# Gate-up groups of a hybrid encoder layer: the order written in the source, and shared banks added in ahead of the last pair

## The chip, the cores and the metric

The kernel runs on one core of a Trainium2 chip. The metric is the device time of one execution in microseconds (us), as the median of several runs; lower is better. Five engines work side by side, each on its own queue of instructions: TensorE (PE; its weight loads are shown apart as PEld), VectorE (DVE), ScalarE (ACT), GpSimd (POOL) and SyncE (SP). Here SP starts nearly all transfers from HBM; POOL starts those that add to what is in SBUF.

## What is computed

One encoder layer in float32, for 256 tokens of width 2048. The change touches the two feed-forward blocks, and of these the first product.

```python
def swiglu(x, w_gate_up, w_down):
    gate, up = jnp.split(x @ w_gate_up, 2, axis=-1)
    return (jax.nn.silu(gate) * up) @ w_down

ff = swiglu(rms_norm(x, pre_norm_ffn1[layer]), w_ffn1_gate_up[layer], w_ffn1_down[layer])
x = x + 0.5 * rms_norm(ff, post_norm_ffn1[layer])
h = rms_norm(x, pre_norm_mix[layer])
... # one projection, a bidirectional recurrence and windowed attention, one projection back
ff = swiglu(rms_norm(x, pre_norm_ffn2[layer]), w_ffn2_gate_up[layer], w_ffn2_down[layer])
x = x + 0.5 * rms_norm(ff, post_norm_ffn2[layer])
```

`w_gate_up` is 2048 x 11264 (gate and up, 5632 columns each), `w_down` 5632 x 2048. All of this is read from HBM once per execution.

## The kernel before

**Three products for one.** TensorE multiplies in a rounded form of float32. Each float32 operand is therefore split into a high part `h` (ScalarE casts it, L176) and a residual `l` (VectorE subtracts, L177), and a product is the sum of three: high by high, high by residual, residual by high. `three` issues these (L442); each multiplies 128 x 128 by 128 x 512. The split of half a raw tile (128 x 1024) is `split_half`; the rings `hip` and `lop` hold five such halves each.

**Groups and pairs.** `Gated` computes gate and up for 512 columns at a time: a group, 11 of them (0 to 10). In a group the contraction over 2048 runs over 8 pairs (u = 0 to 7) of two 128-row slices. The weights of a pair are one raw tile of 128 x 2048 (1 MB, two transfers of 512 KB): four blocks, called b11, b12, b21, b22, two rows k by the columns of gate and of up (n). The results of a group are four PSUM banks `c[m][n]`, with m the half of the tokens; two are of the tag `pa`, two of `pb`, and each tag has four banks.

**Plain and seven-product pairs.** A plain pair makes 8 block products, 24 instructions of TensorE. A pair in `MIXED_IN` makes seven block products instead (Strassen's scheme in Winograd's form), 21 instructions: sums of weight blocks by sums of activations. Two of the seven go straight into c00 and c01, one into c10, and four into shared banks p1, p5, p6, p7, which all such pairs of the group add to. Once in a group `fold` makes from the four shared banks what is still to be added to each of the four c banks: one copy on ScalarE (L530) and eight additions on VectorE (L524 to L547). It does so inside the last pair, whose products are sorted by bank: one addition into a bank, then that bank's six products. With two rooms (`rooms == 2`) the last reads of p5 come late in it (L528). Groups 2 to 10 have four seven-product pairs (2, 3, 4, 6), group 1 has two (2 and 3), since the activation sums of the others are made while it runs; group 0 has none.

**Prepared pairs.** For a seven-product pair, `prepare` runs three or four places ahead (`LEADS`): it loads the raw tile, splits b11 (a short cast and a short residual, 128 x 512), and has POOL start a transfer that reads the other half of the weights a second time and adds it to the first in SBUF (L906). When the pair's turn comes, `seven` splits the lower half, makes two more additions of blocks (L482, L484), splits the upper half, and splits the lower half again. Raw tiles of prepared pairs take turns in three buffers (`rawp`), those of plain pairs in two (`gated.room`).

**After a group** `units` multiplies the silu of the scaled gate (L1017, ScalarE) by the scaled up (L1018, VectorE), transposes the result on TensorE (eight short instructions, L1029, into one bank of each tag), and splits it into `ht`; for the first 8 tiles it also keeps sums of the blocks (`sums_of`, L395 to L399). Its first half runs at the end of the group, its second inside pair 1 of the next one. `put_away` stores some tiles `ht` to HBM from group 2 to 5.

**The order.** Outside of regions marked `manual_schedule`, a planner at build time places every instruction on its engine's queue, by the order in the source as a priority and by its own costs of instructions. The gate-up groups are left to it. Each engine then runs its queue in that order.

Of the kernel before, what the change touches and what calls it, by code (L numbers as in the profile page):

```python
# [20 lines left out]
P = 128  # L21
# [3 lines left out]
KT = D // P  # L25
# [12 lines left out]
def hymba_layer_kernel(  # L38
# [363 lines left out]
    class Blocks:  # L402
# [7 lines left out]
        def __init__(self, tiles, sums):  # L410
            self.tiles, self.sums = tiles, sums
            self.prepared = {}
# [51 lines left out]
        def seven(self, u, aside=None):  # L464

            ready = self.prepared.pop(u, None)
            raw = ready[0] if ready else load(self.source(u))
# [4 lines left out]
            if ready:  # L472
                h, l = ready[1:]
            else:
                h, l = self.one_block()
                split_act(h, l, b11)

                nc.vector.tensor_tensor(
                    four[:, 0:2], four[:, 0::3], four[:, 1:2].to_broadcast([P, 2, 512]), ALU.add
                )  # L480
            lower = split_half(raw, 1)
            nc.vector.tensor_tensor(b22, b11, b22, ALU.add)  # L482
            if ready:
                nc.vector.tensor_tensor(b21, b22, b21, ALU.add)  # L484
            upper = split_half(raw, 0)
            if not ready:
                nc.vector.tensor_tensor(b21, b22, b21, ALU.add)
            if aside:
                aside()
            last = split_half(raw, 1)  # L490
            if not self.p:
# [12 lines left out]
            for at, left, right in (  # L504
                (("p", 0), lhs(0, 0), (h, l)),
                (("c", 0, 0), lhs(1, 0), rhs(lower, 0)),
                (("c", 0, 1), summed(S4), rhs(lower, 1)),
                (("p", 1), summed(S1), rhs(upper, 0)),
                (("p", 3), summed(S3), rhs(upper, 1)),
                (("p", 2), summed(S2), rhs(last, 1)),  # L510
                (("c", 1, 0), lhs(1, 1), rhs(last, 0)),
            ):
                self.three(at, *left, *right)
# [35 lines left out]
        def load_plain(self, u):  # L549
            return load(self.source(u))  # L550

# [7 lines left out]
        def work(self, upto, among=None):  # L559


            while self.pos < upto:
# [8 lines left out]
                else:  # L571
# [4 lines left out]
                    else:  # L576
                        hs, ls = split(self.load_plain(u))
# [276 lines left out]
    MIXED_IN = (2, 3, 4, 6)  # L854
    LEADS = (4, 4, 4, 3)
# [7 lines left out]
    class Gated(Blocks):  # L863
# [7 lines left out]
        def group(self, g, c=None):  # L871
            self.g = g
            self.begin(range(KT // 2), c)

# [7 lines left out]
        def load_plain(self, u):  # L882
            if self.g == 0:
                return load(self.source(u))
            return load(self.source(u), pool=self.room, bufs=2)

        def prepare(self):

            for at, lead in zip(MIXED_IN, LEADS):
                g = self.g  # L890
                if at < lead:
                    at, g = at - lead + KT // 2, g + 1
                else:
                    at -= lead
                u = (at + lead) % (KT // 2)
                if at != self.pos - 1 or g >= NG:
                    continue
                if u not in (self.mixed if g == self.g else self.sums):
                    continue
                src = self.source(u, g)  # L900
                raw = load(src)
                h, l = (
                    self.room.tile([P, 512], F32R, tag=t, name=nm(t), bufs=3) for t in ("h1", "l1")
                )
                split_act(h, l, raw[:, 0:512])
                nc.gpsimd.dma_start(  # L906
                    raw[:, 0:1024].rearrange("p (k c) -> p k c", k=2),
                    src[:, :, 1],
                    accum_op=ALU.add,
                )  # L910
                self.prepared[u] = raw, h, l
# [27 lines left out]
    def ffn(gated, w_dn, post_gain, again, gain=None, lead=None, aside=None):  # L939

        with ExitStack() as st:
# [59 lines left out]
            def folded():  # L1001
                a, b = room_for("z"), room_for("s")
                if gated.g < NG - 1:
                    gated.rooms = 2
                    return [[a, b], [a, b]]
                gated.rooms = 4
                wide = work.tile([P, 2, 512], F32, tag="sp", name=nm("y"), bufs=3)
                return [[a, b], [wide[:, i, :] for i in range(2)]]

            gated.folded = folded  # L1010

            def units(c, scale):

                zs = []
                for m in range(2):
                    z = room_for("zs"[m])
                    nc.scalar.activation(z, c[m][0], AF.Silu, scale=scale[:, m : m + 1])  # L1017
                    nc.vector.scalar_tensor_tensor(  # L1018
                        z, c[m][1], scale[:, m : m + 1], z, ALU.mult, ALU.mult
                    )  # L1020
                    zs.append(z)
                yield
                for j in range(2):
                    bank = (pa, pb)[j]()
                    for i in range(2):
                        for m in range(2):
# [4 lines left out]
                            )  # L1031
                    g = len(hts)
# [11 lines left out]

            pre_stats()
            waiting = None
            for g in range(NG):
                if g:
                    gated.group(g)
                for u in range(gated.pos, KT // 2):  # L1050
                    gated.work(u + 1, (lambda: next(waiting)) if waiting and u == 1 else None)
                    if g == 0:
                        if u == 4:
                            power_and_rest()
                            spread(two)
                        for done in {4: (0, 1, 2), 5: (3, 4), 6: (5, 6), 7: (7,)}.get(u, ()):
                            even(done)
                            if done in MIXED_IN[:2]:
                                sums_in(done)
                        if u == 5 and aside:  # L1060
                            aside()
                    if g == 1 and u in (5, 6):
                        sums_in(MIXED_IN[u - 3])
                    if u == 4 and 1 < g <= AWAY // 2 + 1:
                        put_away(2 * g - 4)
                        put_away(2 * g - 3)
                    gated.prepare()
                waiting = units(gated.c, rest if g else rs2)
                next(waiting)
# [14 lines left out]
            rows.work(2, lambda: next(waiting))  # L1084
# [639 lines left out]
```

## Time and profile before

| | |
|---|---|
| median of 3 runs | 1942.75 us (1942.46 to 1943.67) |
| profiled execution, its own time | 1941.62 us |
| span of the profiled execution | 1939.8 us |
| mean granted TensorE clock | 0.981 |
| bytes moved by DMA | 422.42 MB, 218 GB/s on average |
| packets' time, as a share of 16 DMA engines: started by SP / by POOL | 55.5% / 12.9% |

In lists of waits a row reads: engine, line, what it waited for, microseconds in all, times, the longest. In a timeline a row gives start and duration, and in brackets the idle time ahead of it with what ended it. Rows of instruction groups read: line, engine, operation, out<-in, shapes, count, then busy time and mean nanoseconds of one, then idle time ahead of them and what ended it. In a table of windows each row is a stretch of the span with every engine's busy time, the granted clock (PEclk), the mean busy share of the DMA engines and GB/s.

### The profile page before, as it was taken

What the parts mean: (1) busy time and instruction counts of PE and PEld (TensorE: products, weight loads), DVE (VectorE), ACT (ScalarE), POOL (GpSimd) and SP (SyncE); (2) the same over time, 40 slices, a digit from 0 to 9 for tenths busy, and PEclk for the clock granted to TensorE, in tenths of its full rate; (3) what the DMA queues carried; (4) which work ended last, traced back from release to release, by engine and by line L of the source; (5) the groups of instructions that cost most, each with busy time, mean ns of one, the idle gap of its engine ahead of it and who ended that gap; (6) DMA issues with size and microseconds to landing.
All of it is one profiled execution on the core that took longest, in us unless ns stands there. A gap on an engine that the chain in (4) does not pass through costs nothing.

```text
span 1939.8 us, 23224 instructions
## 1 busy us (share of the span) xinstructions
PE 1859.2 (96%) x8438; PEld 1523.5 (79%) x8438; DVE 1612.7 (83%) x2071; ACT 1113.9 (57%) x1492; POOL 114.4 (6%) x115
## 2 busy tenths in 40 slices
PE   9998899999999999999999999999899989999998
PEld 6776777777788888888888888877777777788886
DVE  7877788887899999667687798977788888899997
ACT  6454555554566566576577566554555555656564
POOL 1100011000000000000000000100000001000000
PEclk9999999999999999999999999999999999999999
DMA  8877777777665566665555457877877777775565
GB/s 295 234 231 227 227 223 225 217 221 215 213 262 204 209 237 234 206 195 156 181 163 157 180 215 253 244 234 230 226 220 214 223 219 219 207 280 196 211 217 190
DMA packets 200019, 422.42 MB, mean 218 GB/s; under 512 B 10984, under 2 KB 45888, under 8 KB 199136
## 3 DMA queue, kind: packets, MB, share of 16 engines
q1 hardware_dynamic: 178880, 380.95, 55.5%
q0 software_dynamic: 21024, 39.99, 12.9%
q8 instruction: 66, 1.08, 0.2%
q14 instruction: 49, 0.40, 0.1%
HBM read 408.29 MB, written 12.60 MB: 217 GB/s over the span
## 4 chain that ended last, share of the span: by engine, by line
PE 58%; DVE 16%; DMA 14%; ACT 7%; issue 4%; POOL 0%; SPq 0%; ACTq 0%; DVEq 0%; POOLq 0%
PE pa L442 22%; PE pb L442 19%; DMA raw<-in_w_ffn_gate_up_dram 13%; DVE l L177 9%; PE pa L309 5%; ACT h L176 5%; PE pa L314 3%; PE pa L364 2%; PE pa L362 2%; PE pa L363 2%; DVE raw L484 1%; DMA raw<-in_w_ffn_down_dram 1%; DVE ht L177 1%; DVE raw L482 0%; DVE s L528 0%
## 5 line engine op out<-in xcount | busy, mean ns | idle before, releaser
L176 ACT CAST h<-raw 128x1024 fp32r<-128x1024 f32 (+1 forms) x861 | 838.0, 1011 | 616.7 <-DMA raw<-in_w_ffn_gate_up_dram 262.2
L177 DVE TENSOR_TENSOR l<-raw,h 128x1024 fp32r<-128x1024 f32 (+1 forms) x861 | 984.7, 1173 | 242.2 <-ACT h L176 214.7
L442 PE MATMUL pa<-h,xt 128*128 128x512 f32 x1104 | 401.8, 406 | 22.0 <-DVE s L528 19.1
L442 PE MATMUL pb<-h,xt 128*128 128x512 f32 x952 | 348.1, 400 | 0.2 <-DVE z L524 0.2
L442 PEld LDWEIGHTS pa<-h,xt 128*128 128x128 f32 x1104 | 215.8, 196 | 77.1 <-DVE s L528 24.9
L442 PE MATMUL pa<-l,xt 128*128 128x512 f32 x552 | 223.4, 405 | 0.0
L442 PEld LDWEIGHTS pb<-h,xt 128*128 128x128 f32 x952 | 183.9, 193 | 39.3 <-DVE z L524 0.6
L442 PE MATMUL pb<-l,xt 128*128 128x512 f32 x476 | 189.0, 397 | 0.0
L442 PE MATMUL pb<-h,ht 128*128 128x512 f32 x464 | 163.5, 390 | 0.0
L442 PE MATMUL pa<-h,ht 128*128 128x512 f32 x464 | 163.1, 389 | 0.0
L442 PE MATMUL pb<-h,xs 128*128 128x512 f32 x304 | 112.4, 401 | 32.8 <-ACT h L176 32.7
L906 POOL DMA_DIRECT2D raw<-in_w_ffn_gate_up_dram x76 | 92.2, 1213 | 851.8 <-DVE l L177 748.0
L442 PEld LDWEIGHTS pa<-l,xt 128*128 128x128 f32 x552 | 108.5, 197 | 24.4 <-DVE l L177 1.9
L309 PE MATMUL pa<-xt,h 128*128 128x512 f32 x512 | 124.5, 393 | 0.2 <-ACT h L176 0.2
L309 PEld LDWEIGHTS pa<-xt,h 128*128 128x128 f32 x512 | 93.8, 188 | 18.7 <-ACT h L176 0.6
L442 PEld LDWEIGHTS pb<-l,xt 128*128 128x128 f32 x476 | 91.6, 192 | 18.9
L442 PE MATMUL pa<-h,xs 128*128 128x512 f32 x304 | 105.9, 389 | 0.0
L442 PEld LDWEIGHTS pa<-h,ht 128*128 128x128 f32 x464 | 87.1, 188 | 18.2
L442 PEld LDWEIGHTS pb<-h,ht 128*128 128x128 f32 x464 | 87.1, 188 | 18.1
L442 PEld LDWEIGHTS pb<-h,xs 128*128 128x128 f32 x304 | 57.8, 190 | 50.3 <-ACT h L176 40.2
L442 PE MATMUL pa<-l,ht 128*128 128x512 f32 x232 | 90.4, 390 | 0.0
L442 PE MATMUL pb<-l,ht 128*128 128x512 f32 x232 | 90.3, 389 | 0.0
(283 smaller groups left out, 2538.7 us busy)
## 6 DMA issues: line engine op xcount, KB each, us to landing
raw<-in_w_ffn_gate_up_dram SPq DMA_DIRECT2D x350, 512.0 KB, 6.1
raw<-in_w_ffn_down_dram SPq DMA_DIRECT2D x88, 1024.0 KB, 5.3
raw<-in_w_mix_in_dram SPq DMA_DIRECT2D x52, 1024.0 KB, 5.1
raw<-in_w_ffn_gate_up_dram POOLq DMA_DIRECT2D x76, 512.0 KB, 6.0
raw<-in_w_mix_out_dram SPq DMA_DIRECT2D x16, 1024.0 KB, 5.0
away<-ht SPq DMA_DIRECT2D x16, 512.0 KB, 6.0
ht<-away SPq DMA_DIRECT2D x16, 512.0 KB, 7.0
pg<-in_post_norm_ffn_dram SPq DMA_DIRECT2D x4, 512.0 KB, 7.3
```

The source lines that it names most:

```text
L176: nc.scalar.copy(hi, src)
L177: nc.vector.tensor_tensor(lo, src, hi.bitcast(F32), ALU.subtract)
L309: nc.tensor.matmul(slot[f], weights(hs, kk, f), xcol(xt, k), start=(k == 0), stop=(k == KT - 1))
L314: nc.tensor.matmul(slot[f][:, 0:T], weights(ls, kk, f), xcol(xt, kh * 8 + kk, 0), start=False, stop=False,)
L362: nc.tensor.matmul(dst, xh, h[:, o : o + n], start=(k == 0), stop=False)
L363: nc.tensor.matmul(dst, xh, l[:, o : o + n], start=False, stop=False)
L364: nc.tensor.matmul(dst, xl, h[:, o : o + n], start=False, stop=(k == KT - 1))
L442: nc.tensor.matmul(self.bank(at), lhs, rhs, start=(n == 1), stop=n in (ends, self.of[at]), skip_group_check=n > ends,)
L484: nc.vector.tensor_tensor(b21, b22, b21, ALU.add)
L906: nc.gpsimd.dma_start(raw[:, 0:1024].rearrange("p (k c) -> p k c", k=2), src[:, :, 1], accum_op=ALU.add,)
```

## The change

The groups from 1 on are issued inside `manual_schedule`, which fixes on every engine the order in which the source issues instructions. The source therefore now writes that order out.

- `plan` lists all pairs of groups 1 to 10 in two kinds, mixed (seven-product) and plain, and loads three mixed and two plain raw tiles. Afterwards `load_next` issues the next load of a kind as soon as the last split of a tile of that kind is issued.
- `splits` issues a pair's splits in steps, `take` gives or issues its products. In most of the group (`pair_ahead`) the first two splits of pair u + 1 stand ahead of the products of pair u, and the third behind them.
- `prepare` of the four mixed pairs stands, in this order: for the first, while pair 6 of the group before is at work; for the second and third, in `first_pairs` before the products of pair 0; for the fourth, ahead of the products of pair 3.
- `boundary` takes the place of the fold inside the last pair, with one order written out for ScalarE, VectorE and TensorE: the additions into c00 and c10 come first, and p5 is read for the last time ahead of the addition into c11. The first split of the next group's pair 0 stands between the additions.
- `units` has finer steps: the two silus at the boundary, the multiplications at the start of the next group, the transposes behind pair 0, the evacuation among the splits of pair 2.
- The seven-product pairs are 2, 4, 5 and 6, and in group 1 they are 2 and 4.

The last group's fold is written apart and keeps four rooms. `seven` loses its branch for prepared pairs, and its products become a function of their own, `products`.

```diff
-    MIXED_IN = (2, 3, 4, 6)
-    LEADS = (4, 4, 4, 3)
+    MIXED_IN = (2, 4, 5, 6)
...
+        def plan(self):
+            self.here = {g: MIXED_IN if g > 1 else MIXED_IN[:2] for g in range(1, NG)}
+            self.kinds = {True: [], False: []}
+            for g in range(1, NG):
+                for u in range(KT // 2):
+                    self.kinds[u in self.here[g]].append((g, u))
+            self.raws, self.firsts, self.split_of = {}, {}, {}
+            for mixed in (False, True, False, True, True):
+                self.load_next(mixed)
+
+        def load_next(self, mixed):
+            if self.kinds[mixed]:
+                g, u = self.kinds[mixed].pop(0)
+                kw = {} if mixed else {"pool": self.room, "bufs": 2}
+                self.raws[g, u] = load(self.source(u, g), **kw)
...
+        def splits(self, g, u):
+            raw = self.raws[g, u]
+            got = self.split_of[g, u] = []
+            if (g, u) in self.firsts:
+                b11, b12, b21, b22 = (raw[:, i * 512 : (i + 1) * 512] for i in range(4))
+                got.append(split_half(raw, 1))
+                nc.vector.tensor_tensor(b22, b11, b22, ALU.add)
+                nc.vector.tensor_tensor(b21, b22, b21, ALU.add)
+                yield
+                got.append(split_half(raw, 0))
+                yield
+                got.append(split_half(raw, 1))
+                self.load_next(True)
+            else:
+                got.append(split_half(raw, 0))
+                yield
+                got.append(split_half(raw, 1))
+                self.load_next(False)
+            yield
...
+            def boundary(g):
+                a, b = room_for("z"), room_for("s")
+                c, (p1, p5, p6, p7) = gated.c, gated.p
+                add = nc.vector.tensor_tensor
+                rest_of = gated.take(g, last)
+
+                def bank(m, n):
+                    for k in range(2):
+                        rest_of[4 * k + 2 * m + n]()
+
+                nc.scalar.copy(a, p1)
+                add(c[0][0], c[0][0], a, ALU.add)
+                ahead = gated.splits(g + 1, 0)
+                next(ahead)
+                add(b, p6, a, ALU.add)
+                add(a, p7, b, ALU.add)
+                add(c[1][0], c[1][0], a, ALU.add)
+                bank(0, 0)
+                bank(1, 0)
+                add(b, p5, b, ALU.subtract)
+                add(c[0][1], c[0][1], b, ALU.add)
+                bank(0, 1)
+                add(b, p5, a, ALU.subtract)
+                add(c[1][1], c[1][1], b, ALU.add)
+                bank(1, 1)
+                next(ahead)
+
+            def first_pairs(g, waiting):
+                gated.group(g)
+                some(waiting, 1)
+                gated.prepare(g, MIXED_IN[1])
+                some(waiting, 1)
+                ahead = gated.splits(g, 1)
+                some(ahead, 2)
+                gated.prepare(g, MIXED_IN[2])
+                for one in gated.take(g, 0):
+                    one()
+                some(waiting, 1)
+                ahead = gated.splits(g, 2)
+                some(ahead, 2)
+                some(waiting, 1)
+                some(ahead, 1)
+                for one in gated.take(g, 1):
+                    one()
+
+            def pair_ahead(g, u):
+                ahead = gated.splits(g, u + 1)
+                next(ahead)
+                if u + 1 == MIXED_IN[1]:
+                    gated.prepare(g, MIXED_IN[3])
+                next(ahead)
+                for one in gated.take(g, u):
+                    one()
+                for _ in ahead:
+                    pass
+                if g == 1 and u in (4, 5):
+                    sums_in(MIXED_IN[u - 2])
+                if u == 5 and 1 < g <= AWAY // 2 + 1:
+                    put_away(2 * g - 4)
+                    put_away(2 * g - 3)
+
+            waiting = units(gated.c, rs2)
+            some(waiting, 2)
+            with tc.manual_schedule():
+                gated.prepare(1, MIXED_IN[0])
+                some(gated.splits(1, 0), 2)
+                for g in range(1, NG):
+                    first_pairs(g, waiting)
+                    for u in range(2, last - 1):
+                        pair_ahead(g, u)
+                    if g < NG - 1:
+                        ahead = gated.splits(g, last)
+                        some(ahead, 2)
+                        gated.prepare(g + 1, MIXED_IN[0])
+                        for one in gated.take(g, last - 1):
+                            one()
+                        boundary(g)
+                        waiting = units(gated.c, rest)
+                        some(waiting, 2)
```

More of the change, by code (lines that the diff above doesn't have):

```diff
@@ L880, in left_sums @@
             return self.sums[u]
[L882 to L911, printed above, removed]
@@ L1031, in units @@
                             )
+                yield
+                for bank in banks:
                     g = len(hts)
@@ L1043, in units, with some @@
                 yield
+            def some(steps, n):
+                for _ in range(n):
+                    next(steps)
             pre_stats()
[L1046 to L1069, printed above, removed]
@@ new lines, in ffn @@
+            some(gated.splits(NG - 1, last), 2)
+            gated.take(NG - 1, last - 1)
+            a, b = room_for("z"), room_for("s")
+            wide = work.tile([P, 2, 512], F32, tag="sp", name=nm("y"), bufs=3)
+            gated.folded = lambda: [[a, b], [wide[:, i, :] for i in range(2)]]
+            fold = gated.fold()
+            final = gated.take(NG - 1, last)
+            for m in range(2):
+                for n in range(2):
+                    next(fold)
+                    for k in range(2):
+                        final[4 * k + 2 * m + n]()
@@ L1070, in ffn @@
+            for _ in fold:
+                pass
+            waiting = units(gated.c, rest)
+            some(waiting, 4)
             room_cm.__exit__(None, None, None)
@@ L1083, in ffn @@
             rows.work(1)
-            rows.work(2, lambda: next(waiting))
+            rows.work(2, lambda: some(waiting, 2))
             for i, u in enumerate((1, 3, 0, 5, 2, 7, 4, 6)):
```

95 lines of the change are left out of this document (65 added, 30 removed).

## Prediction

> **What bounds the kernel now.** I read the page first, then the chain of waits of TensorE, then TensorE's timeline around the gate-up groups, and last a table of windows, one for each group.
>
> ```profile
> span 1939.8 us, 23224 instructions
> ...
> PE 1859.2 (96%) x8438; PEld 1523.5 (79%) x8438; DVE 1612.7 (83%) x2071; ACT 1113.9 (57%) x1492; POOL 114.4 (6%) x115
> ```
> ```profile
> PE pb L442 <- ACT h L176: 33.0, 16, 3.2
> PE pa L442 <- DVE s L528: 19.1, 11, 4.1
> PE pb L442 <- DVE l L177: 10.6, 15, 0.8
> ```
>
> TensorE is busy 96% of the span, and what it waits for is nearly all of L442 (the products of the three-term scheme): 62.7 us in three rows. These are casts (L176) and residuals (L177) that come late, and one subtraction of the fold (L528), after which a bank comes free. A busy TensorE is not one at its peak, so I take its pace from the timeline and the chain, and its clock from the windows.
>
> ```profile
> 291.09 2.72 PE pa L442 x12
> ```
> ```profile
> 113.89 0.28 PE L1029 MATMUL pa<-ident,z 128*128 128x128 f32 x1
> ...
> 114.68 0.47 PE L442 MATMUL pb<-h,xt 128*128 128x512 f32 x1
> ```
> ```profile
> 281.37 0.50 PE L442 MATMUL pb<-h,xs 128*128 128x512 f32 x1 [2.65 <-ACT h L176]
> 282.63 0.65 PE L442 MATMUL pb<-l,xs 128*128 128x512 f32 x1 [0.76 <-DVE l L177]
> ...
> 283.50 0.63 PE L442 MATMUL pb<-h,xt 128*128 128x512 f32 x1
> 283.93 0.63 PE L442 MATMUL pb<-l,xt 128*128 128x512 f32 x1
> ```
>
> Twelve products take 2.72 us, 0.227 each. The eight transposes of a group take 114.68 - 113.89 = 0.79. After the gap of 2.65 + 0.76 us the products start 283.93 - 283.50 = 0.43 us apart: half pace for a while, so a gap costs more than its idle time. The transposes (L1029) stand once in every group, so the time from one set to the next is a group's period.
>
> ```profile
> core 0: us, PE busy (x) PEld busy (x) DVE busy (x) ACT busy (x) POOL busy (x), PEclk, DMA share, GB/s
> ...
> 308.66:356.57 47.91, 44.23 (x189) 35.59 (x188) 39.04 (x49) 25.21 (x30) 4.84 (x4) 0.96 0.77 222
> ...
> 500.99:543.59 42.60, 42.39 (x189) 34.39 (x188) 37.38 (x43) 24.49 (x30) 1.20 (x1) 1.00 0.64 218
> ...
> 1523.24:1571.36 48.12, 43.11 (x189) 34.30 (x188) 38.81 (x48) 25.23 (x30) 4.84 (x4) 1.00 0.76 216
> ...
> 1667.35:1709.71 42.36, 42.14 (x189) 34.46 (x188) 37.37 (x43) 24.49 (x30) 1.20 (x1) 1.00 0.64 220
> sum 859.68, PE 795.90 PEld 639.22 DVE 695.29 ACT 452.13 POOL 79.80; mean PE 44.22 PEld 35.51 DVE 38.63 ACT 25.12 POOL 4.43
> ```
>
> These are the 18 periods that end groups 2 to 10 of both feed-forward layers. Each holds 180 products (4 pairs of 24, 4 of 21) and 8 transposes: 180 x 0.227 + 0.8 = 41.6 us. The last period of each layer takes 42.60 and 42.36, so the floor is real. The other 16 take 859.68 - 42.60 - 42.36 = 774.7 us, 48.4 each: 6.8 us over the floor, 109 us in all, of 1941.6 us that the profiled execution took (its span and 1.8 around it; the median of the runs is 1.1 above it). No other engine fills a period: DVE 39.0 of 47.9, ACT 25.2, the transfers 0.77 x 47.9 = 36.9.
>
> Why TensorE waits is seen at ScalarE in the period from 308.66:
>
> ```profile
> L177 DVE TENSOR_TENSOR l<-raw,h 128x1024 fp32r<-128x1024 f32 x21 | 24.7, 1220 | 2.9 <-ACT h L176 2.9
> L176 ACT CAST h<-raw 128x1024 fp32r<-128x1024 f32 x20 | 19.8, 1047 | 5.5 <-DVE pa L541 3.7 <-DVE raw L484 1.4 <-DMA raw<-in_w_ffn_gate_up_dram 0.3
> ...
> L177 DVE TENSOR_TENSOR l<-raw,h 128x512 fp32r<-128x512 f32 x4 | 2.8, 690 | 5.8 <-ACT h L176 5.8
> ...
> L176 ACT CAST h<-raw 128x512 fp32r<-128x512 f32 x4 | 2.5, 621 | 14.2 <-DMA raw<-in_w_ffn_gate_up_dram 14.2
> ...
> L541 DVE TENSOR_TENSOR pa<-pa,s 128x512 f32<-128x512 f32 x1 | 0.7, 689 | 0.0
> ```
> ```profile
> 326.60 5.35 ACT L176 CAST h<-raw 128x512 fp32r<-128x512 f32 x6 [5.32 <-DMA raw<-in_w_ffn_gate_up_dram]
> ```
>
> The four short casts are those of `prepare`, for a pair three or four places on. ScalarE stands 14.2 us per period before them, each time for a load, and the long casts of the pair that TensorE wants next stand behind. At 326.60 it has stood 5.32 us and then makes six casts in a row; TensorE waits meanwhile.
>
> **The change part by part.** *What stays.* The count of products, casts, residuals, adds, transposes and bytes is the same: four seven-product pairs from group 2 on, two in group 1. Pairs 2, 4, 5, 6 for 2, 3, 4, 6 cost nothing by themselves. All that moves is the order.
>
> *Early casts and loads.* Loads now go out as soon as the buffer's last split is issued, three mixed and two plain ones ahead. Their prices:
>
> ```profile
> raw<-in_w_ffn_gate_up_dram SPq DMA_DIRECT2D x350, 512.0 KB, 6.1
> ...
> raw<-in_w_ffn_gate_up_dram POOLq DMA_DIRECT2D x76, 512.0 KB, 6.0
> ...
> ht<-away SPq DMA_DIRECT2D x16, 512.0 KB, 7.0
> ```
>
> For pairs 2, 4 and 5 a load has a pair or more of TensorE's time (4.8 to 5.4 us each) beyond its 6.1 us before its cast is next on ScalarE; I cost those casts' wait at nothing. Pair 6 is the tight one: its load goes out after pair 2's last split, and its cast stands in ScalarE's queue between the first and the second split of pair 4, so ScalarE may stand there about 3 us, with pair 4's other two splits and then pair 5's behind it. What hides that is TensorE's own pair 3 (5.4 us) and the first 9 products of pair 4 (2.0 us), which need neither split. The whole link is load 6.1 + cast 0.62 + residual 0.69 + accumulating transfer 6.0 = 13.4 us until DVE may add pair 6's blocks. Its room: pairs 2 to 5 take 21 + 24 + 21 + 21 products, 19.7 us; the adds must be done about 0.9 us before pair 6 starts (9 of its products run meanwhile, 2.0 us, less add, cast and residual, 0.69 + 1.05 + 1.22); pair 2's last split is 0 to 3.4 us (15 products) into pair 2. That leaves 15.4 to 18.8: slack of 2.0 to 5.4 us. SP takes its issues in order, but its order is that of the splits, so no load waits for a later buffer; in groups 2 to 5 two stores of `put_away` stand ahead of the load of the next group's pair 1, and I put 0.2 us a period for all that queues.
>
> *The boundary.* The first products of a group no longer wait for L528: the last read of p5 now stands ahead of the add into c11, and the last six products wait for that add. In its place come four waits of TensorE, one ahead of each bank's six products. With five halves in the ring, the second split of pair 7 takes the room of pair 5's last half, which is free when TensorE starts pair 6. From there: cast 1.05, residual 1.22, residual of the early cast 0.69, first add 0.69, residual of the next group's pair 0 1.22, three adds 2.07 = 6.9 us until c10 is ready. TensorE comes there after 21 + 6 products, 6.1 us. So it waits 0.8; each later bank has 1.38 us of adds against 1.36 of products. No row shows this wait: from 0.4 (neighbouring instructions overlap a little) to 1.9 (ScalarE's copy and the next split late by one cast); below nothing it can't be, since the floor is counted in full. I take 0.9, near the sum.
>
> *Transposes and evacuation* move behind pair 0. They need both banks multiplied by the scale, some 2 us after the last product, and pair 0 gives 5.4: free.
>
> *Group 1* has six plain pairs on two buffers. One turn is load 0.6 + 6.1, two splits of 1.22 and a cast, about 10.2, against two pairs of 5.44 = 10.9. From 0 to 7 us per layer; I take 3, near the row of the windows where DMA is fullest:
>
> ```profile
> 66.00:114.00 48.00, 47.00 (x211) 38.54 (x209) 43.66 (x58) 24.66 (x29) 3.66 (x3) 1.00 0.91 278
> 1235.00:1280.00 45.00, 44.23 (x201) 36.32 (x200) 39.74 (x54) 23.95 (x29) 3.68 (x3) 1.00 0.87 268
> ```
>
> There TensorE loses 1.0 and 0.8 us now. Group 0 and the last group's fold keep their course.
>
> *Sum.* A period becomes 41.6 + 0.9 + 0.2 = 42.7 us; 774.7 - 16 x 42.7 = 91.5 gained. Group 1 gives back 2 x 3 - 1.8 = 4.2. 1941.6 - 87.3 = 1854.3, and 1.1 up to the median: 1855 us. At 0.4 us a boundary, with nothing lost to queues or in group 1, it is 1941.6 - (774.7 - 16 x 42.0) - 1.8 + 1.1 = 1838.
>
> **The rivals.** *Half pace at each boundary.* Short waits, several in a row, might drop the clock as the gap at 281 did.
>
> ```profile
> 1543.05 0.50 PE L442 MATMUL pb<-h,xs 128*128 128x512 f32 x1 [2.44 <-ACT h L176]
> 1544.31 0.50 PE L442 MATMUL pb<-l,xs 128*128 128x512 f32 x1 [0.76 <-DVE l L177]
> ```
> ```profile
> 1566.69 0.50 PE L442 MATMUL pa<-h,xt 128*128 128x512 f32 x1 [1.78 <-DVE s L528]
> ```
>
> The period from 1523.24 holds these three gaps, and its clock is 1.00; in that from 308.66 it is 0.96. So 2.4 + 0.8 us may still go free, and waits of under 1 us should. If not: 0.04 x 47.9 = 1.9 us at lost clock for each period, 16 x 1.9 = 30 more, 1885. Chance 0.05. The Trainium skill, TensorE: Matmul & The Clock Gate, "A second HAM failure mode: psum-queue depth-cycling", speaks for this rival: going round the PSUM banks makes TensorE idle for moments and its clock swing. The clock of 1.00 from 1523.24 speaks against it here.
>
> *Loads late.* The same transfers in less time: 36.9 of 42.7 us is a share of 0.86. With landings of 8.5 us the link of pair 6 is 18.3, up to 2.9 late; a period is 45.6, the gain 774.7 - 730 - 4 = 41, 1902. Against it: group 1 ran at a share of 0.91 and lost 1.0. Chance 0.18, from just over the forecast to about 1925.
>
> *Slower: ScalarE's fixed queue stands for pair 6.* The same link with landings doubled by a full queue: 12.1 + 1.3 + 12.0 = 25.4, late by 6.6 to 10.0; a period of 42.7 + 8.3 = 51, 1941.6 + 16 x 2.6 + 4 = 1988. It decides against the change once a period passes 48.4, thus from 5.7 us late: landings of 10 to 12 us. Nothing can be put ahead in a fixed order, as the 14.2 us before four casts shows already; but the rows of whole layers stand at 6.0 to 7.0. Chance 0.07. The Trainium skill, PSUM — Partial Sum Buffer, "Engine vs sequencer instructions", calls the queues of ScalarE and VectorE strictly first in, first out; the six casts in a row at 326.60 agree.
>
> *No effect:* the gaps move and none goes, 1943. It would need a bound other than order near 48, and none of the engines' rows has one. Chance 0.02.
>
> **How the numbers follow.** The forecast has 0.68, from 1838 to 1880. Faster is forecast, half pace and late loads: 0.91; same, 0.02; slower, 0.07. A measurement of this kernel tells 0.2% (4 us) from no change. The range from 1837 to 1898 takes in half pace and some half of late loads; above it lie about 0.09 + 0.09.
>
> **What would show it.** Right: periods of 42 to 43.5 us with clock 1.00 and a DMA share near 0.86; the waits of L442 for L176 and for the last read of p5 gone, and in their place one of about 1 us in each group for the add into c10; ScalarE's idle time before short casts down from 14 us a period to about 3, all for pair 6. Wrong: TensorE waiting inside pairs 4 to 6 for a residual (late loads), products 0.43 us apart after a boundary (half pace), or periods of 48 with ScalarE idle for loads.

## The result, and the profile after

The changed kernel takes 1852.26 us (median of 4 runs, 1851.13 to 1853.72), against 1942.96 for the kernel before: a ratio of 0.953, with a 95% interval from 0.952 to 0.955. The forecast was 1855, the range 1837 to 1898. The page, and TensorE's longest waits:

```profile
span 1849.5 us, 23264 instructions
...
PE 1816.7 (98%) x8438; PEld 1504.2 (81%) x8438; DVE 1628.2 (88%) x2071; ACT 1127.2 (61%) x1492; POOL 114.3 (6%) x115
```
```profile
PE pb L441 <- DVE pb L1118: 17.5, 18, 1.6
PE pb L441 <- DVE l L177: 1.5, 2, 0.8
```

TensorE has the same 8438 instructions as before. Of the 90 us, 48 are idle time (span less busy time: 80.6 before, 32.8 now) and 42 are busy time (1859.2 before). About 25 us of the 42 are half pace that is gone: before, 138 products started 0.40 to 0.46 us behind the one ahead with no stop between; now 12 do. The three waits that led the list before are gone from the groups (the second row above lies behind them). One is left there, 18 times: the products of c10 (L441, as `pb`) for the add into c10 (L1118), once in each boundary of groups 1 to 9 in both layers. The windows from transposes to transposes:

```profile
core 0: us, PE busy (x) PEld busy (x) DVE busy (x) ACT busy (x) POOL busy (x), PEclk, DMA share, GB/s
...
150.27:194.30 44.03, 42.35 (x189) 34.35 (x188) 41.07 (x49) 27.25 (x33) 4.85 (x4) 1.00 0.92 266
194.30:237.18 42.88, 42.06 (x190) 34.45 (x189) 38.92 (x47) 24.90 (x30) 4.84 (x4) 1.00 0.93 272
...
366.11:408.98 42.87, 42.05 (x189) 34.46 (x188) 39.88 (x48) 26.06 (x30) 4.82 (x5) 1.00 0.88 243
...
451.88:495.61 43.73, 43.73 (x199) 36.30 (x197) 39.33 (x46) 26.16 (x31) 1.71 (x2) 1.00 0.82 261
...
sum 775.41, PE 760.54 PEld 623.80 DVE 715.11 ACT 466.06 POOL 80.91; mean PE 42.25 PEld 34.66 DVE 39.73 ACT 25.89 POOL 4.49
```

The clock is 1.00 in every window, and most periods are 42.87 us. The last one of each layer (43.73) holds nine products more than before (189 against 180), since it starts at the transposes of the group before, which now stand behind pair 0 and no longer nine products into pair 1. TensorE is busy all through it. Without these two the 16 periods make 687.9 us, against 774.7: 86.8 of the 90 us.

One boundary, TensorE and then VectorE (start, duration):

```profile
306.39 0.39 PE L441 MATMUL pa<-h,xt 128*128 128x512 f32 x1
...
312.28 0.39 PE L441 MATMUL pa<-h,xt 128*128 128x512 f32 x1
313.49 0.50 PE L441 MATMUL pb<-h,xt 128*128 128x512 f32 x1 [0.82 <-DVE pb L1118]
313.83 0.39 PE L441 MATMUL pb<-l,xt 128*128 128x512 f32 x1
```
```profile
309.49 0.69 DVE L1113 TENSOR_TENSOR pa<-pa,z 128x512 f32<-128x512 f32 x1
310.09 1.22 DVE L177 TENSOR_TENSOR l<-raw,h 128x1024 fp32r<-128x1024 f32 x1
311.22 0.68 DVE L1116 TENSOR_TENSOR s<-pb,z 128x512 f32<-128x512 f32 x1
311.94 0.69 DVE L1117 TENSOR_TENSOR z<-pb,s 128x512 f32<-128x512 f32 x1
312.74 0.70 DVE L1118 TENSOR_TENSOR pb<-pb,z 128x512 f32<-128x512 f32 x1
```

This is the queue the forecast added up: c00, the residual of the next pair 0, two sums, c10. Pair 6 starts on TensorE at 306.39, and the add into c10 ends at 312.74 + 0.70 = 313.44: 7.05 us, against 6.9 in the forecast. TensorE comes 0.82 us too early. ScalarE's short casts, and the transfers:

```profile
L176 ACT CAST h<-raw 128x512 fp32r<-128x512 f32 x4 | 2.5, 618 | 2.3 <-DMA raw<-in_w_ffn_gate_up_dram 2.3
```
```profile
raw<-in_w_ffn_gate_up_dram SPq DMA_DIRECT2D x350, 512.0 KB, 5.3
...
raw<-in_w_ffn_gate_up_dram POOLq DMA_DIRECT2D x76, 512.0 KB, 8.3
```

In the period from 280.34 ScalarE stands 2.3 us before short casts (14.2 in the period shown before the change), all ahead of one of the four. Over the 18 periods now it is 0.2 to 3.9 us; over the 16 that were long before it was 8.1 to 15.7. Loads land sooner in the median than before, the accumulating transfers 2.3 us later.

### The profile page after: what moved, and what is told of

Its sections match the earlier page's. It is cut to its first block, busy times and chain, and to the rows that moved or that the text cites. A ratio compares the mean times of both kernels' runs of the same rounds, so it can differ in the third digit from the quotient of the medians.

```text
span 1849.5 us, 23264 instructions
## 1 busy us (share of the span) xinstructions
PE 1816.7 (98%) x8438; PEld 1504.2 (81%) x8438; DVE 1628.2 (88%) x2071; ACT 1127.2 (61%) x1492; POOL 114.3 (6%) x115
## 3 DMA queue, kind: packets, MB, share of 16 engines
q8 instruction: 66, 1.08, 0.2%
## 4 chain that ended last, share of the span: by engine, by line
PE 70%; DVE 14%; DMA 8%; ACT 4%; issue 3%; SPq 1%; POOL 0%; DVEq 0%; ACTq 0%; POOLq 0%
PE pa L441 28%; PE pb L441 25%; DVE l L177 8%; DMA raw<-in_w_ffn_gate_up_dram 6%; PE pa L309 5%; PE pa L314 3%; ACT h L176 3%; PE pa L364 2%; PE pa L363 2%; PE pa L362 2%; DMA raw<-in_w_ffn_down_dram 2%; DVE pb L1118 1%; DVE z L1117 1%; DVE pa L1113 1%; DVE s L1116 1%
## 5 line engine op out<-in xcount | busy, mean ns | idle before, releaser
L176 ACT CAST h<-raw 128x1024 fp32r<-128x1024 f32 (+1 forms) x861 | 846.7, 1013 | 454.2 <-PE pb L441 113.2
L441 PE MATMUL pa<-h,xt 128*128 128x512 f32 x1104 | 387.5, 392 | 0.2
L441 PE MATMUL pb<-h,xt 128*128 128x512 f32 x952 | 341.1, 393 | 17.5 <-DVE pb L1118 17.5
L441 PEld LDWEIGHTS pa<-h,xt 128*128 128x128 f32 x1104 | 207.4, 188 | 44.3 <-DVE xt L232 0.6
L441 PEld LDWEIGHTS pb<-h,xt 128*128 128x128 f32 x952 | 178.6, 188 | 64.4 <-DVE pb L1118 25.1
L441 PE MATMUL pa<-l,xt 128*128 128x512 f32 x552 | 215.7, 391 | 0.0
L441 PE MATMUL pb<-l,xt 128*128 128x512 f32 x476 | 185.5, 390 | 0.0
L441 PE MATMUL pb<-h,ht 128*128 128x512 f32 x464 | 163.5, 390 | 0.0
L441 PE MATMUL pa<-h,ht 128*128 128x512 f32 x464 | 162.7, 389 | 0.0
L441 PEld LDWEIGHTS pa<-l,xt 128*128 128x128 f32 x552 | 103.9, 188 | 20.6 <-DVE l L177 0.7
L441 PE MATMUL pa<-h,xs 128*128 128x512 f32 x304 | 105.9, 389 | 0.0
L441 PE MATMUL pb<-h,xs 128*128 128x512 f32 x304 | 105.9, 389 | 0.0
L441 PEld LDWEIGHTS pb<-l,xt 128*128 128x128 f32 x476 | 89.4, 188 | 17.1
L441 PEld LDWEIGHTS pa<-h,ht 128*128 128x128 f32 x464 | 87.1, 188 | 18.2
L441 PEld LDWEIGHTS pb<-h,ht 128*128 128x128 f32 x464 | 87.1, 188 | 18.1
L441 PE MATMUL pb<-l,ht 128*128 128x512 f32 x232 | 90.3, 389 | 0.0
L441 PE MATMUL pa<-l,ht 128*128 128x512 f32 x232 | 90.3, 389 | 0.0
L314 PE MATMUL pa<-xt,l 128*128 128x256 f32 x512 | 69.1, 285 | 0.0
```

Of the source, the lines that this page charges most:

```text
L176: nc.scalar.copy(hi, src)
L314: nc.tensor.matmul(slot[f][:, 0:T], weights(ls, kk, f), xcol(xt, kh * 8 + kk, 0), start=False, stop=False,)
L441: nc.tensor.matmul(self.bank(at), lhs, rhs, start=(n == 1), stop=n in (ends, self.of[at]), skip_group_check=n > ends,)
```

## The experiments

Runs marked "one execution" have no interval of their own; the runs of one kernel lie within 0.1 to 0.4% of each other.

**The first split of the next pair 0 moved behind c10.**

```diff
                 add(c[0][0], c[0][0], a, ALU.add)
-                ahead = gated.splits(g + 1, 0)
-                next(ahead)
                 add(b, p6, a, ALU.add)
                 add(a, p7, b, ALU.add)
                 add(c[1][0], c[1][0], a, ALU.add)
+                ahead = gated.splits(g + 1, 0)
+                next(ahead)
```

> The first split of the next group's pair 0 is moved from behind the add into c00 to behind the add into c10; all else is as in the changed kernel. Theory (the 0.8 to 1.6 us that TensorE waits in each group for the add into c10 is the sum of VectorE's queue from the start of pair 6): the sum up to c10 falls by the 1.22 us residual to 5.7 us, under the 6.1 us of products, so that wait goes; but the residual now stands ahead of the add into c01, 5.7 + 1.22 + 1.38 = 8.3 us against 7.5 us of products, so a wait of about 0.8 us comes up there and the time stays at 1852, within 4 us. Rival (an add into a bank between its products costs TensorE by itself): the wait stays at c10, the time too. Rival (the sum is too long by more than the trace shows in idle time, and there is slack at c01): no wait at either, 1835.

Measured: 1859.43 us (ratio 0.957, 0.955 to 0.959), periods of 43.46. TensorE's timeline in one boundary:

```profile
314.27 0.50 PE L441 MATMUL pb<-h,xt 128*128 128x512 f32 x1 [0.27 <-DVE pb L1116]
...
316.73 0.50 PE L441 MATMUL pa<-h,xt 128*128 128x512 f32 x1 [0.81 <-DVE pa L1122]
```

The wait moved to c01 (here L1122), with 0.8 us, as VectorE's queue said. But 0.27 stayed at c10, and the time rose by 7 where none was expected: 1.08 us of idle time in two stops for 0.82 in one lengthened the period by 0.59. So two short stops cost more than one longer one.

**Both splits of the next pair 0 behind the eight adds.** As above, but `splits(g + 1, 0)` stands behind `bank(1, 1)`, both steps together.

> Both splits of the next group's pair 0 are moved behind the last of the eight shared adds. Theory (VectorE's queue): c10 is ready at 5.7 us from the start of pair 6 against 6.1 of products, c01 at 7.1 against 7.5, c11 at 8.5 against 8.8, and the first residual of pair 0 at 9.7 against 10.2. No wait is left in the 18 boundaries, 17.5 us go, the time is 1835, a period 41.9 to 42.0. Rival (an add into a bank between its products costs by itself): 1852, the wait at c10 stays. Rival (the splits come too late): a wait of about 0.5 to 1 us before the first products of pair 0 takes the place of the one before, 1843 to 1852.

Measured: 1841.72 us (0.948, 0.946 to 0.950), most periods 42.3. The wait fell to 0.28 in most boundaries and did not go. VectorE's timeline shows what the sum had left out:

```profile
349.73 0.69 DVE L1113 TENSOR_TENSOR pa<-pa,z 128x512 f32<-128x512 f32 x1
350.90 0.69 DVE L1114 TENSOR_TENSOR s<-pb,z 128x512 f32<-128x512 f32 x1 [0.49 <-PE pb L441]
```

VectorE now comes early and stands for p6, which is ready only after 18 of pair 6's 21 products. From there three dependent adds are longer than the 9 products that TensorE still has. So the time fell by 10.5 us, and not by the 17.5 expected.

**p6 ahead of p7 in pair 6**, on top of that kernel.

```diff
+            if u == self.p6_early:      # the group's last seven-product pair
+                steps[4], steps[5] = steps[5], steps[4]
+            for at, left, right in steps:
                 self.three(at, *left, *right)
```

> On top of the kernel with both splits of the next pair 0 behind the eight shared adds: in pair 6 the products for p6 stand ahead of those for p7, so p6 is ready after 15 of the 21 products and not after 18. Theory (the 0.3 us wait for c10 that is left there begins at p6: VectorE stands 0.49 us for it and then makes three adds): p6 is ready 0.68 us earlier, c10 too, and the wait of 0.28 goes, with the 0.4 us that each stop of TensorE costs beside its idle time (periods of 42.32 with 0.28 of idle time over a floor of 41.6): 18 x 0.7 = 13 us, 1829, periods of 41.6 to 41.8. Rival (TensorE stops at each bank whatever VectorE does): 1842.

Measured: 1837.44 us (0.946, 0.945 to 0.948). TensorE's waits:

```profile
PE pb L442 <- DVE pb L1121: 4.7, 10, 0.9
...
PE pa L442 <- DVE pa L1118: 1.3, 3, 0.6
```

Where nothing else is late the periods are 41.8 us and TensorE stops nowhere in them: it doesn't stop at a bank as such. The periods of groups 3 to 6 kept 42.3 to 43.5, 8.6 us over 41.8 in sum, which is why it is 1837 and not 1829.

**The old order of the shared adds**, in the changed kernel.

```diff
+                add(b, p6, a, ALU.add)
                 add(c[0][0], c[0][0], a, ALU.add)
                 ahead = gated.splits(g + 1, 0)
                 next(ahead)
-                add(b, p6, a, ALU.add)
                 add(a, p7, b, ALU.add)
-                add(c[1][0], c[1][0], a, ALU.add)
-                bank(0, 0)
-                bank(1, 0)
                 add(b, p5, b, ALU.subtract)
+                bank(0, 0)
                 add(c[0][1], c[0][1], b, ALU.add)
-                bank(0, 1)
                 add(b, p5, a, ALU.subtract)
+                bank(0, 1)
+                add(c[1][0], c[1][0], a, ALU.add)
+                bank(1, 0)
                 add(c[1][1], c[1][1], b, ALU.add)
```

> One part undone: the order written out stays, but the boundary goes back to the order of adds that the fold had before (c00, c01, c10, c11, each bank's products behind its add, with the sums for two banks made in between). Theory (VectorE's queue sets the boundary): the add into c00 now waits for p6, which is ready 18 products into pair 6, and two more sums stand ahead of c01; from the start of pair 6 c00 is ready at 5.7 us against 4.8, c01 at about 9.0 against 7.1. TensorE waits some 2.9 us in each boundary in place of 1.0, 18 x 1.9 = 34 more: 1886; with a drop of the clock after it, as the 3.4 us gap before had, up to 30 more. Rival (the new order of the adds brings nothing, only the written order and the loads do): 1852, within 4.

Measured, one execution: 1878.29 us, periods of 44.61. The waits of TensorE, for the adds into c01 (L1120) and c00 (L1114):

```profile
PE pa L441 <- DVE pa L1120: 26.5, 18, 1.5
PE pa L441 <- DVE pa L1114: 14.0, 16, 0.9
```

1.7 us more a period, 26 in all where 34 were expected: the order of the adds is worth that much. The clock stayed at 1.00 in every period.

**The short cast of pair 6 earlier.**

```diff
                 some(ahead, 1)                      # pair 2's last split
+                gated.prepare(g, MIXED_IN[3])
                 for one in gated.take(g, 1):
...
-                if u + 1 == MIXED_IN[1]:
-                    gated.prepare(g, MIXED_IN[3])
```

> One step moved: the short cast of pair 6 and its accumulating transfer stand right behind pair 2's last split, where its load has only just been issued, and no longer between the splits of pair 4. Theory (what the kernel before lost was ScalarE standing for a load with the casts of the next pair behind it): ScalarE stands some 5 to 6 us there in the 18 groups from group 2 on, pair 3's first split comes 2 to 3 us after TensorE wants it, the period goes to about 45.5, and where the gap passes 3 us the clock drops too: 1852 + 18 x 2.7 = 1900, up to 1935 with the clock. The idle time of ScalarE before short casts goes from 2.3 us a period to 5 or more. Rival (the place of that cast is of no weight; loads ahead and the boundary made the gain): 1852, within 4.

Measured, one execution: 1924.07 us. ScalarE stands 6.87 us for the load in the period shown, and TensorE then stops twice ahead of pair 3:

```profile
359.77 1.56 ACT L176 CAST h<-raw 128x512 fp32r<-128x512 f32 x2 [6.87 <-DMA raw<-in_w_ffn_gate_up_dram]
```
```profile
361.39 0.49 PE L441 MATMUL pa<-h,xt 128*128 128x512 f32 x1 [0.87 <-ACT h L176]
362.65 0.50 PE L441 MATMUL pa<-l,xt 128*128 128x512 f32 x1 [0.77 <-DVE l L177]
```
```profile
PE pa L441 <- ACT h L176: 27.5, 18, 3.1
PE pb L441 <- DVE pb L1118: 21.6, 18, 1.6
PE pa L441 <- DVE l L177: 13.4, 18, 0.8
```

One cast put too early, with the accumulating transfer behind it, gives back 72 us, most of the gain: 41 us of idle time for pair 3's splits, and half pace again (mean clock 0.988, against 0.999 in the changed kernel).

**The fixed order alone**, in the kernel before.

```diff
+            written = ExitStack()
             for g in range(NG):
+                if g == 1:
+                    written.enter_context(tc.manual_schedule())
...
+            written.close()
```

> One part alone: the kernel before, with the groups from 1 on inside a region that fixes every engine's order to that of the source as it stood, and nothing else. Theory (what counts is which order is written, and the change's gain lies in its loads ahead, its late early casts and its boundary): ScalarE no longer stands for loads, since SP runs ahead in the source's order; but at the boundary the adds keep the old order (3.0 us over the floor, as the kernel with the old fold has it: 44.61 against 41.6), and the next group's pair 0 is split only behind the silus and multiplications, some 2 us after TensorE's last product. A period of 46 to 47 us without a drop of the clock, some 48.5 with one: 1915 to 1945. Rival (any order fixed in the source cures what the planner did): periods of 43 to 44.6, 1852 to 1880.

Measured, one execution: 2004.96 us, periods of 49 to 52 (one of 57), slower than the planner's order and 60 us past the expected end. TensorE's stops in one period:

```profile
179.05 0.50 PE L442 MATMUL pa<-l,xt 128*128 128x512 f32 x1 [0.34 <-DVE l L177]
...
181.63 0.50 PE L442 MATMUL pa<-l,xs 128*128 128x512 f32 x1 [0.92 <-DVE l L177]
...
192.72 0.50 PE L442 MATMUL pa<-l,xs 128*128 128x512 f32 x1 [0.94 <-DVE l L177]
...
214.10 0.50 PE L442 MATMUL pa<-h,xt 128*128 128x512 f32 x1 [2.55 <-ACT h L176]
215.49 0.50 PE L442 MATMUL pa<-l,xt 128*128 128x512 f32 x1 [0.89 <-DVE l L177]
```

The expected stop for the next pair 0 is there (2.55 + 0.89), and half pace behind it. What the expectation missed is that seven-product pairs, split one behind the other, come late inside the group too; and the old order of the adds, which it counted at 3 us, causes no stop here, presumably since TensorE is late anyway. Fixing an order brings nothing by itself.

**Pairs 2, 3, 4, 6 again**, in the new order.

> One part undone: the seven-product pairs are 2, 3, 4, 6 again (2 and 3 in group 1), in the new order, with the early cast of pair 6 at its place among pair 4's splits. Theory (which four pairs they are costs nothing by itself, only where the early casts and loads fall): periods within 0.5 us of 42.9, the time 1852, within 8. Rival (the choice of pairs carries part of the gain, since three such pairs in a row at 2, 3, 4 give VectorE 3 x 5.3 us of work against 3 x 4.8 of products right behind the boundary, where it has no lead): TensorE waits 1 to 2 us inside pair 3 or 4, 1870 to 1890.

Measured, one execution: 1849.04 us, every one of the 16 periods between 42.82 and 42.87. ScalarE's short casts from 107 to 488 us:

```profile
L176 ACT CAST h<-raw 128x512 fp32r<-128x512 f32 x33 | 20.3, 614 | 0.0
```

They wait for nothing, where in the changed kernel they wait 16.4 us over the same stretch. The choice of pairs brought no gain; the three long periods of the changed kernel (44.03, 43.16, 43.42) go with it. In these three ScalarE stands 3.9, 3.1 and 3.3 us for pair 6's load, in the other 15 up to 2.4.

**More traffic**: eight copies of 256 KB in each group, whose results nothing reads.

```diff
+                for k in range(2):
+                    dose = dram.tile([P, 512], F32, tag=f"dose{u}{k}", name=nm("dose"))
+                    nc.sync.dma_start(dose, gated.source(u, g)[:, k, 0])
```

> The changed kernel with 2 MB of added traffic in each group from 1 on: eight copies of 256 KB from the weights to a scratch place in HBM, two behind each of pairs 2 to 5, started by SP. Nothing reads them. Theory: the work of the transfers, 0.88 to 0.93 of 42.9 us and some 6 us more, is then 44 to 46 us a period, more than TensorE's 41.6, so that DMA sets the pace: share near 1, periods of 44 to 46.5, ScalarE standing for loads of all kinds and not for pair 6 alone, 1875 to 1910, with drops of the clock up to 1940. Rival (the fixed queue of ScalarE makes it worse than the transfers' work, as landings double): periods over 48, slower than the kernel before. Rival (late loads are no matter): 1852 to 1860.

Measured, one execution: 1868.72 us. Two of its windows:

```profile
107.39:150.28 42.89, 42.06 (x190) 34.48 (x189) 35.94 (x44) 22.55 (x26) 4.06 (x4) 1.00 1.01 303
...
240.13:287.34 47.21, 43.15 (x189) 34.22 (x188) 40.89 (x48) 26.31 (x32) 4.84 (x4) 1.00 0.98 298
```

Late loads begin here: the share is about 1 in all eight windows of the first layer, yet periods go from 42.9 to 47.2, 16 us in all, less than the 23 that were the least expected. In the second layer the share is about 1 in every period too. Seven of the 16 periods stay at 42.9 to 43.0, those of groups 2, 8 and 9 among them; all of groups 3 to 6, where the stores' price falls (last experiment), are longer. So the share alone doesn't set the period, and the changed kernel is not far from this bound, and not at it.

**Pairs 2, 3, 4, 6 on top of p6 early.**

> The kernel with p6 early and the next pair 0 split last, and the seven-product pairs 2, 3, 4, 6 in it. Theory (the 0.6 to 1.7 us by which the periods of groups 2 to 5 stand over 41.8 there come from ScalarE standing 3 to 4.4 us before pair 6's short cast; with these pairs that wait was nothing in any period): all periods from group 2 on at 41.8 to 42.0, the 16 of them 8 us less in sum, group 1 up to 1 us more in each layer: 1828 to 1832. Rival (those groups lose by their DMA share of 0.92 to 0.94, from the stores, whatever the pairs): 1837, periods of 42.3 to 43.5 stay.

Measured: 1841.23 us (0.948, 0.946 to 0.949). The short casts of groups 2 to 8 of the first layer wait for nothing again, yet groups 3 to 6 keep periods of 42.2 to 44.4. My theory for these groups fell.

**The two stores behind the load of the next pair 1**, on top of p6 early with pairs 2, 4, 5, 6.

```diff
-                if u == 5 and 1 < g <= AWAY // 2 + 1:     # pair_ahead
-                    put_away(2 * g - 4)
-                    put_away(2 * g - 3)
...
                         some(ahead, 2)                     # splits of pair 7, with that load
+                        if 1 < g <= AWAY // 2 + 1:
+                            put_away(2 * g - 4)
+                            put_away(2 * g - 3)
```

> On top of the kernel with p6 early (pairs 2, 4, 5, 6): in groups 2 to 5 the two stores of put_away are issued behind the load of the next group's pair 1, and no longer just ahead of it. Theory (those periods stand 0.6 to 1.7 us over the other groups' 41.8 because that load lands 10 to 12 us after its issue behind the stores, and ScalarE then stands 2.8 and 1.5 us before pair 1's casts, which uses up VectorE's lead up to the boundary): that load lands in 6 to 8 us, ScalarE's waits there go, the eight periods come down to 41.8 to 42.3, 6 to 8 us in sum: 1829 to 1832. Rival (their DMA share of 0.92 to 0.94 makes every transfer late, whichever stands first): the wait moves to other loads, periods of 42.3 to 43.5 stay, 1837.

Measured: 1831.34 us (0.943, 0.941 to 0.944), the fastest of all. The stores go out late in groups 2 to 5, so their price falls on groups 3 to 6. The period of group 5, first in the kernel with p6 early, then here:

```profile
234.40:277.54 43.14, 42.34 (x189) 34.36 (x188) 39.86 (x48) 26.10 (x32) 4.84 (x4) 1.00 0.93 269
```
```profile
232.56:274.74 42.18, 42.05 (x190) 34.46 (x189) 39.91 (x49) 26.30 (x31) 4.84 (x4) 1.00 0.94 279
```

The share is as high, the period 1 us shorter. In the earlier kernel ScalarE stands for pair 1's load just at its start:

```profile
231.50 1.05 ACT L176 CAST h<-raw 128x1024 fp32r<-128x1024 f32 x1 [2.81 <-DMA raw<-in_w_ffn_gate_up_dram]
234.00 2.52 ACT L176 CAST h<-raw 128x1024 fp32r<-128x1024 f32 x3 [1.46 <-DMA raw<-in_w_ffn_gate_up_dram]
```

Behind the stores that load landed 10.0 and 11.9 us after its issue; ahead of them 5.6 and 6.9 (it is two transfers), and the stand is gone. All periods from group 2 on are now 41.8 to 42.4, but for the last of each layer with its nine products more. By which step the late load lengthened the period is not shown: in the periods of groups 3 to 6 ScalarE's stand for pair 6 shrank with it, from 3.3 to 4.4 us to 1.7 to 3.2.

What the loads going out earlier, the splits one pair ahead and the transposes behind pair 0 are worth, each alone, no run shows. The parts don't add up either: 72 us for one cast's place and 26 for the order of the adds are more than the whole gain of 90.

## Why the prediction was right

*The floor and what stood over it.* Right: 109 us were named, 87 came back in the 16 periods. That part of the loss was pace and not idle time was read from products 0.43 us apart, and the profile after bears it out: 42 us less busy time for the same instructions, some 25 of it half pace.

*ScalarE standing for early loads.* Right: the rows of before show the stand, 14.2 us in one period, and moving one cast in the new order shows its price, 72 us. That the written order and not the fixing of an order makes the gain was not said in the prediction; the kernel with the fixed order alone shows it.

*The boundary.* The wait for c10 was put at 0.9 us and is 17.5 / 18 = 0.97. The forecast sum was the right queue: it comes to 6.9 us and took 7.05, and the wait moved to c01 with a residual. But a stop of 0.82 shown takes 1.05 us of the period (42.87 against 41.82 without a stop). This is the term that was too small: 42.7 forecast, 43.0 measured on average (687.9 / 16). The sum also left out that p6 itself is late. In the changed kernel that costs nothing, since VectorE comes to p6 at 311.22 without a wait; it counts once the residual is out of the way.

*The link of pair 6.* The link held in 13 of 16 periods, though not with the prices of the sum: ScalarE stood there 1.6 us on average and not 3, loads took 5.3 us and not 6.1, and the accumulating transfers took 8.3 us and not 6.0, at a DMA share of 0.88 to 0.94 where 0.86 was forecast. The three long periods, two in the first layer and one in the second, are those where it stood over 3 us. "Pairs 2, 4, 5, 6 cost nothing by themselves" was off by 2 to 3 us.

*The stores.* Named as standing ahead of the next pair 1's load, and put at 0.2 us a period. No run moves the stores in the changed kernel itself. Its three long periods, 2.0 us over the others in sum, lie in groups 3, 5 and 6, where the stores' price falls; with the boundary's wait gone, moving the stores is worth 6 us. The 0.2 agrees by chance with something else: the periods without a stop are 41.8 and not 41.6, in groups 7 to 9 too, where no stores go out.

*Groups 0 and 1.* Here luck brought the sum close. The 3 us a layer for two plain buffers did not come: counted by TensorE's products, group 1 takes 0.4 us longer in the first layer and 2.0 in the second, its boundary and 0.9 us at the second layer's transposes included. Group 0, which the forecast left as it was, ends 4.8 us earlier in the first layer, mostly since one stop and the half pace behind it are gone. Before:

```profile
49.97 0.25 PE L119 MATMUL pb<-ident,rows 72*128 72x72 f32 x1 [2.24 <-DMA rows<-in_hgrn_out_norm_dram]
```

All runs with the written order lack this stop; the kernel before with a fixed order has it (2.33 us). Why it went is not shown. So the 16 periods brought 4.7 us less than forecast and the rest of the program 7.7 more, two errors against each other, and the sum came out 3 us from the result.

*The rivals.* Half pace at each boundary did not occur: clock 1.00 with one stop in every boundary, and with two in the kernel with the old adds. The Trainium skill, TensorE: Matmul & The Clock Gate, "A second HAM failure mode: psum-queue depth-cycling", tells of another kernel whose clock swings because TensorE is idle for short moments, often, as it goes round the PSUM banks. One or two stops of up to 1.6 us in a period of 43 to 45 us showed no such swing here. Late loads as a bound on the whole period appear only with 2 MB more a group, and then not in every group. The slower case, ScalarE's fixed queue, was produced only with a cast in the wrong place, and even that ended at 1924.

## What to carry to other kernels

When an engine with a fixed queue has to wait for a transfer, everything behind it waits: put an instruction that needs a load where the load has landed, and look for what stands behind it. Before writing out an order, add up each engine's queue between two fixed points, name the wait that will be left, and check also when each of the queue's inputs is ready. A stop costs more than the idle time that the profile shows, so two short ones can cost more than one longer one.

## What the runs showed of the hardware

A stop of TensorE costs some 0.2 to 0.3 us beside its idle time in the profile. In the boundary shown the product before the stop starts at 312.28 and counts as busy for 0.39, though the next could start 0.23 later; after the stop the second product starts 313.83 - 313.49 = 0.34 behind the first. That is 0.16 + 0.11 us. The periods agree: 0.28 of idle time gives 42.32 against 41.82, 0.27 + 0.81 gives 43.46.

At a share near 1, 289 to 306 GB/s, the transfers still fed seven of 16 periods at the pace of the changed kernel. The order of a few issues on SP's queue mattered: with two stores ahead of a load its two transfers landed 10.0 and 11.9 us after their issue, with the stores behind it 5.6 and 6.9.

The length of a gap alone did not decide whether the clock fell. The stop of 2.24 us at 49.97 was followed by a granted clock of 0.50 for 3.41 us. In the kernel with the early cast these two were followed by the same, and their period has 0.96:

```profile
407.58 0.50 PE L441 MATMUL pa<-h,xt 128*128 128x512 f32 x1 [1.07 <-ACT h L176]
408.84 0.50 PE L441 MATMUL pa<-l,xt 128*128 128x512 f32 x1 [0.76 <-DVE l L177]
```

The 2.44 + 0.76 us at 1543 in the kernel before, with 1.78 more in the same period, left it at 1.00.
